# Two longer reckoned times in the planner of a hybrid decoder layer: low parts of weights on VectorE, wide operations on GpSimd

## The chip, the cores and the metric

The kernel runs on one core of a Trainium2 chip. A core has five engines, each with a queue of its own that it works through in order: TensorE (PE in the profile; its weight loads are PEld), VectorE (DVE), ScalarE (ACT), GpSimd (POOL) and SyncE (SP), which issues the weight transfers. The engines wait for each other by semaphores. The metric is the device time of one execution in microseconds; the figure before is the median of three runs.

## The reference, cut to what matters

One layer with 256 tokens of width 1024. A conditioning vector gives six vectors of shift, scale and gate. The normalised input goes through one product with 7168 columns, which feeds a convolution branch, an attention branch and two gates; their gated sum goes through `w_out`. Then 64 small experts, eight for each token, and a shared one.

```python
mod = c_act @ w_ada[l] + b_ada[l]                       # sh1, sc1, g1, sh2, sc2, g2
h = rms_norm(x, norm1_g[l]) * (1 + sc1) + sh1
ca, cb, q, k, v, gate_conv, gate_attn = jnp.split(h @ w_in[l], offsets, axis=-1)
u = causal_depthwise_conv(ca * sigmoid(cb), 31 taps) + b_dw
y_conv = silu(layer_norm(u)) @ w_pw2 + b_pw2
a = softmax(q1 k1) - lam * softmax(q2 k2)               # 8 heads, causal
y_attn = rms_norm(a @ v, subln_g)
x = x + g1 * ((sigmoid(gate_conv) * y_conv + sigmoid(gate_attn) * y_attn) @ w_out[l])
h2 = rms_norm(x, norm2_g[l]) * (1 + sc2) + sh2
x = x + g2 * moe_ffn(h2, ...)                           # top 8 of 64 experts, one shared
```

All is float32.

## The kernel before, in words

**How it is laid out.** The program has two parts. In the first, the weights of `w_in`, `w_pw2` and `w_out` come in 18 chunks of 512 columns (the list `SEQ`: `i0` to `i13`, `p0`, `p1`, `o0`, `o1`), each in eight blocks of 128 rows, which makes 144 work items. In the second, the experts' weights (3 MB for each expert) are streamed through slots of 1 MB. The first six experts are fixed; which weights come after them is known only when the routing has ordered the experts by their load, in `order_ids` (`ids`, line 1364).

**Split weights.** To multiply at float32 accuracy with a faster matmul, each weight block is split in two: ScalarE casts it to a high part (line 795), and a subtraction gives the low part (`lo_part`, line 776), on GpSimd or on VectorE. TensorE then runs twelve matmuls for an item (lines 802 to 804 for outputs with tokens in rows, 811 to 813 for outputs with channels in rows). Four buffers of high and low parts (two in the tile `ra`, two in `rb`) are in use up to the chunk `p1`, eight for the last two chunks.

**The convolution** (`conv`, lines 859 and 863) runs on VectorE: for each of four pairs of channel blocks one first tap and 30 more for each block, 248 instructions in all, accumulating in a PSUM bank; the last tap of a pair is written to `fa`. `layer_norm` adds up the channels (lines 1102 and 1108), subtracts the mean (1115), squares on ScalarE (1117), adds the squares (1125), takes the root on GpSimd (1132), broadcasts it over TensorE (1135, 1138), scales (1143), applies SiLU on ScalarE (1149) and splits the result into parts for the product with `w_pw2` (1152, 1154).

**Attention** (`attn`) runs in six groups: scores on TensorE (1012, 1016), row maxima on VectorE (1023), exponentials on ScalarE (1027), reciprocals and the factor lambda (1031, 1034, 1037), the combination of both softmaxes on VectorE (1040), transposes (1046) and their copy (1049), the product with v (1057), squares (1066), sums and root (1069, 1071, 1073), scaling (1075), transposes (1079), the gate (1084).

**What sets the order.** A planner written in Python (`Plan`) runs when the kernel is built. Each piece of work is a generator that yields requests: an engine with a time that the planner reckons for it (`GT(n)` for a GpSimd operation of n columns, `TT(n)` for a two-input operation on VectorE, and so on), an event or a buffer. The planner keeps a clock for each engine, takes the request that can start first by its own clock (with priorities `PRIO` among those that start within 0.02 us), and writes the instruction out; so the reckoned times set the order in every engine's queue. Where a request names two engines, the one that would be done first is taken, with a penalty if one is given: `lo_part` asks for GpSimd or VectorE, and VectorE gets a penalty of 1.0 us (`LO_BIAS`) once the convolution's second block of input is ready. `conv` has the lowest priority. The emitted queues are fixed; on the chip an engine that reaches an instruction whose input is late waits, with all that is behind it.

`GT(n)` is used for the low parts of weights (512 columns), the gain of q and k (line 928), the sums of the layer norm (256), the merge of the two branches, the residual sums and the split of the normalised tokens. `TT(512)` is 0.07 + 0.00104 x 512 = 0.60 us.

Of the kernel before, what the change touches and what calls it, by code (L numbers as in the profile page):

```python
# [166 lines left out]
LO_BIAS, Q_BIAS = (0.0, 1.0), 3.0  # L167
# [4 lines left out]
def TT(n):  # L172
    return "D", 0.07 + 0.00104 * n
# [16 lines left out]


def GT(n):
    return "G", 0.15 + 0.0021 * n


def MM(n):
# [4 lines left out]
def tile_hybrid_block(ctx, tc, x, c, positions, w_ada, b_ada, norm1_g, w_in, conv_dw, conv_dw_b,  # L201
# [4 lines left out]
    P, T, D, K = 128, 256, 1024, 8  # L206
# [6 lines left out]
    pl = Plan()  # L213
# [218 lines left out]
    def done(key, q, now=None):  # L432
        now = pl.cur.ready if now is None else now
        w = loaded[key]
        if w.off[q] in halves:
            e = halves.pop(w.off[q])
            load(*e, [1], now)
            advance(now)
        elif w.off[q] in once:
            once.remove(w.off[q])  # L440
        elif w.off[q] == LAST:
            w2s.close()
            obs = ctx.enter_context(tc.tile_pool(name="obs", bufs=1)).tile([P, 8 * KB], F32R, name="obs")
            pl.put("ob", *(ob_of(obs[:, i * D:(i + 1) * D]) for i in range(2)))
        else:
            pl.pools["w"].append((now, w.off[q]))
            advance(now)
# [324 lines left out]
    step = [0]  # L772

    def lo_part(i, hl, w, k):
        e = yield [GT(512), TT(512) + (None, LO_BIAS[pl.ev("u", 1).t is not None])]
        (nc.gpsimd if e == "G" else nc.vector).tensor_tensor(hl[:, 1], w.k[k], hl[:, 0].bitcast(F32),  # L776
                                                             op=OP.subtract)
        pl.set("hl", i)
        w.left[k // 4] -= 1
        if not w.left[k // 4]:  # L780
            done(w.key, k // 4)
# [4 lines left out]
    def splits(chunks):  # L786
        for i, (c_, k) in enumerate(items):
            key = chunks[c_][0]
            yield pl.ev("L", *key, k // 2)
            w = loaded[key]  # L790
            w.left, w.key = [4, 4] if not k else w.left, key
            yield w.at[k]
            hl = yield Get("hl")
            yield AS(512)
            nc.scalar.copy(hl[:, 0], w.k[k])  # L795
            pl.events["buf", i] = hl
            pl.spawn(lo_part(i, hl, w, k))
# [98 lines left out]
    def fin_qk(which, half):  # L896
        def qk_out(o, t):
# [23 lines left out]
            else:  # L921
# [3 lines left out]
            pl.put("s8", sm_)  # L925
            yield pl.ev("angles")
            e = yield [GT(512), TT(512) + (None, Q_BIAS)]
            (nc.gpsimd if e == "G" else nc.vector).tensor_tensor(
                q3, q3, qkg[:, which, None, :].to_broadcast([P, 8, 64]), op=OP.mult)
# [167 lines left out]
    def layer_norm():  # L1097
        yield pl.ev("cv", 0)
        for k in range(1, 6):
            yield pl.ev("cv", k)  # L1100
            e = yield [GT(256), TT(256) + (None, LO_BIAS[1])]
            (nc.gpsimd if e == "G" else nc.vector).tensor_tensor(lns, lns if k > 1 else cv[:, 0], cv[:, k], op=OP.add)
# [898 lines left out]
```

## Time and profile before

| | us |
|---|---|
| median of three runs (818.65 to 822.19) | 820.47 |
| the profiled execution | 819.49 |
| its span, from the first to the last instruction | 817.7 |
| TensorE busy | 766.1 (94%) |
| VectorE busy | 444.6 (54%) |
| ScalarE busy | 324.9 (40%) |
| GpSimd busy | 192.4 (24%) |

The profile shows one execution. Its shares are means over both parts of the program: 271.04 MB are moved in the span, at 420 GB/s or so in the second part and at 155 to 365 GB/s in the first. A busy TensorE is not one at its peak, since matmul ends are modelled. In the timelines an instruction can begin before the one ahead of it has ended, so durations add up to more than the time seen as busy. Times inside a run are counted from the start of the span.

### The profile page before, as it was taken

How to read it: one execution, taken by the hardware profiler on the slowest of the kernel's cores; microseconds unless marked ns; L12 is line 12 of the kernel's file. 1: busy time of each engine (PE TensorE's matmuls, PEld its weight loads, DVE VectorE, ACT ScalarE, POOL GpSimd, SP SyncE). 2: the span in 40 equal slices, each digit the busy share in tenths (PEclk: the TensorE clock that was granted, in tenths of full speed). 3: DMA queues.
4: the chain of work that ended last, by engine and by line, in shares of the span. 5: the costliest groups of instructions: out<-in, count | busy, mean ns of one | idle time of the engine just before them, and what ended most of it. 6: DMA issues, size and time to landing. Idle time of an engine off the chain costs nothing.

```text
span 817.7 us, 13180 instructions
## 1 busy us (share of the span) xinstructions
PE 766.1 (94%) x4759; PEld 469.8 (57%) x4759; DVE 444.6 (54%) x1035; ACT 324.9 (40%) x713; POOL 192.4 (24%) x246
## 2 busy tenths in 40 slices
PE   3999999899996999999999797999999999999997
PEld 2898777589784987545454141354464455444543
DVE  5458998999996677433433141344344344433443
ACT  4356656865759755223221021232232232232220
POOL 3003788888572693000002000000000000000000
PEclk9999999899997999989999898999999999999999
DMA  9998776546654676469999999999999999999993
GB/s 312 365 336 288 261 253 227 180 161 227 228 184 155 239 280 252 165 245 390 390 420 420 422 421 420 421 422 420 420 421 422 421 420 421 420 421 419 419 413 139
DMA packets 69883, 271.04 MB, mean 331 GB/s; under 512 B 6085, under 2 KB 15893, under 8 KB 46520
## 3 DMA queue, kind: packets, MB, share of 16 engines
q1 hardware_dynamic: 69464, 270.00, 84.9%
q8 instruction: 38, 0.62, 0.3%
q0 software_dynamic: 304, 0.16, 0.1%
q14 instruction: 29, 0.24, 0.1%
q10 hardware_dynamic: 48, 0.01, 0.0%
HBM read 269.11 MB, written 1.05 MB: 330 GB/s over the span
## 4 chain that ended last, share of the span: by engine, by line


## 5 line engine op out<-in xcount | busy, mean ns | idle before, releaser
L1802 PE MATMUL bank<-fa 128*32 128x512 f32 (+2 forms) x1048 | 203.7, 608 | 8.3 <-DMA fa<-in_w_exp_gu_dram 8.3
L1802 PEld LDWEIGHTS bank<-fa 128*32 128x32 f32 (+2 forms) x1048 | 60.3, 124 | 132.1 <-issue 107.3
L863 DVE SCALAR_TENSOR_TENSOR bank<-fa,tap,bank 128x256 f32<-128x256 f32 x232 | 112.9, 486 | 6.1
L1676 DVE SCALAR_TENSOR_TENSOR fa<-bank,gsc,h 128x256 f32<-128x256 f32 x28 | 13.5, 484 | 170.1 <-ACT h L1672 170.1
L1849 PE MATMUL bank<-fa 128*32 128x512 f32 (+1 forms) x496 | 83.9, 596 | 0.0
L1672 ACT ACTIVATE h<-bank 128x256 f32<-128x256 f32 x28 | 10.8, 385 | 179.7 <-PE bank L1802 179.7
L776 POOL TENSOR_TENSOR rb<-fa,rb 128x512 fp32r<-128x512 f32 x46 | 60.2, 1317 | 65.6 <-ACT rb L795 64.6
L1694 DVE TENSOR_TENSOR fa<-bank,fa 128x512 f32<-128x512 f32 x54 | 37.4, 692 | 65.5 <-PE bank L1849 62.7
L776 POOL TENSOR_TENSOR ra<-fa,ra 128x512 fp32r<-128x512 f32 x48 | 63.9, 1339 | 20.5 <-ACT ra L795 17.1
L1762 ACT CAST obs<-fa 128x512 fp32r<-128x512 f32 x54 | 33.4, 618 | 83.7 <-DVE fa L1694 83.7
L1719 DVE TENSOR_TENSOR fa<-fa,bank 128x512 f32<-128x512 f32 x108 | 66.7, 678 | 0.0
L1491 ACT ACTIVATE fa<-bank,b2c,a2c 128x256 f32<-128x256 f32 x108 | 53.6, 561 | 20.8 <-PE bank L1523 20.8
L795 ACT CAST ra<-fa 128x512 fp32r<-128x512 f32 x76 | 46.8, 622 | 37.0 <-PE bank L812 22.9
L1523 PE MATMUL bank<-ra 128*128 128x256 f32 x448 | 60.5, 288 | 0.0
L1710 PE MATMUL bank<-obs,ra 128*128 128x512 f32 x216 | 58.3, 412 | 0.0
L795 ACT CAST rb<-fa 128x512 fp32r<-128x512 f32 x68 | 42.0, 623 | 37.8 <-PE bank L812 22.4
L1802 PE MATMUL bank<-late_w,fa 128*32 128x512 f32 (+2 forms) x168 | 51.9, 627 | 4.1 <-DMA late_w<-in_w_exp_gu_dram 4.1
L1523 PEld LDWEIGHTS bank<-ra 128*128 128x128 f32 x448 | 55.6, 191 | 0.2
L1710 PEld LDWEIGHTS bank<-obs,ra 128*128 128x128 f32 x216 | 38.7, 188 | 28.8 <-issue 21.5
L811 PE MATMUL bank<-ra 128*128 128x256 f32 x160 | 47.8, 299 | 1.9 <-ACT ra L577 1.8
L1849 PEld LDWEIGHTS bank<-fa 128*32 128x32 f32 (+1 forms) x496 | 22.8, 119 | 41.1 <-issue 35.3
L811 PE MATMUL bank<-ra,rb 128*128 128x256 f32 x160 | 46.1, 288 | 0.0
(376 smaller groups left out, 1391.5 us busy)
## 6 DMA issues: line engine op xcount, KB each, us to landing
fa<-in_w_exp_gu_dram SPq DMA_DIRECT2D x100, 1024.0 KB, 19.8
fa<-in_w_exp_down_dram SPq DMA_DIRECT2D x50, 1024.0 KB, 19.8
fa<-in_w_ada_dram SPq DMA_DIRECT2D x24, 1024.0 KB, 7.9
fa<-in_w_in_dram SPq DMA_DIRECT2D x22, 1024.0 KB, 5.3
late_w<-in_w_exp_gu_dram SPq DMA_DIRECT2D x17, 1024.0 KB, 19.3
late_w<-in_w_exp_down_dram SPq DMA_DIRECT2D x12, 1024.0 KB, 6.8
fa<-in_w_exp_gu_dram SPq DMA_DIRECT2D x22, 512.0 KB, 9.4
fa<-in_w_in_dram SPq DMA_DIRECT2D x12, 512.0 KB, 9.4
```

What stands on the lines that cost most here:

```text
L776: (nc.gpsimd if e == "G" else nc.vector).tensor_tensor(hl[:, 1], w.k[k], hl[:, 0].bitcast(F32), op=OP.subtract)
L795: nc.scalar.copy(hl[:, 0], w.k[k])
L811: nc.tensor.matmul(o, hl[:, 0, mm], src_t[:, k, 0], start=(k == 0 and m % 2 == 0), stop=False)
L863: nc.vector.scalar_tensor_tensor(cv[:, m] if j == TAPS - 1 else acc, u_sb[:, m, j:j + T], tap[:, m, j:j + 1], acc, op0=OP.mult, op1=OP.add)
L1491: nc.scalar.activation(xt[:, k, 0:ns], p3[:, f2, 0:ns], AF.Identity, bias=b2c[:, k:k + 1], scale=a2c[:, k:k + 1])
L1523: nc.tensor.matmul(p3[:, f2, 0:ns], xr[:, a, t, (f + f2) * P:(f + f2 + 1) * P], tables[b0][:, t, 0:ns], start=(f2 + t + a == 0), stop=(f2 ...
L1694: nc.vector.tensor_tensor(o32, pd[h], g2b[:, h * 512:(h + 1) * 512], op=OP.mult)
L1710: nc.tensor.matmul(p, info.pT[:, t * P:(t + 1) * P], ob[a], start=(a == 0), stop=(a == 1))
L1719: nc.vector.tensor_tensor(x_sb[:, t, d], x_sb[:, t, d], p, op=OP.add)
L1762: nc.scalar.copy(ob[0], o32)
L1802: nc.tensor.matmul(pg[o:o + m], info.xt[:, k, o:o + m], loaded["g", js[e]].k[k], start=(k == 0), stop=(k == K - 1))
L1849: nc.tensor.matmul(pd[h][o:o + m], info.aT[:, f, o:o + m], loaded["d", js[e]].k[f][:, h * 512:(h + 1) * 512], start=(f == 0), stop=(f == 1))
```

## The change

Two numbers that the planner reckons with are changed. A GpSimd operation of n columns is taken to last 0.15 + 0.0023 n us, where it was 0.15 + 0.0021 n: 1.33 in place of 1.23 us for 512 columns, 0.74 in place of 0.69 for 256. The low part of a weight block on VectorE is taken to last 0.85 us, where it was 0.60; its penalty stays. No instruction is added or taken out by hand; the planner writes another order.

```diff
@@ -190,7 +190,7 @@
 def GT(n):
-    return "G", 0.15 + 0.0021 * n
+    return "G", 0.15 + 0.0023 * n
@@ -772,7 +772,7 @@
     def lo_part(i, hl, w, k):
-        e = yield [GT(512), TT(512) + (None, LO_BIAS[pl.ev("u", 1).t is not None])]
+        e = yield [GT(512), ("D", 0.85) + (None, LO_BIAS[pl.ev("u", 1).t is not None])]
         (nc.gpsimd if e == "G" else nc.vector).tensor_tensor(hl[:, 1], w.k[k], hl[:, 0].bitcast(F32),
                                                              op=OP.subtract)
```

In the new order 56 of the 144 low parts are on VectorE, where there were 50, and four operations of 256 columns go the same way (one of line 1102, one of 1125, two of 1154). ScalarE loads its function tables three times less. SyncE's queue is the same. From the residual sums on (line 1202), the queues differ by one scaling of tokens (line 1237) and its neighbours. Between the first of the convolution and the layer norm nearly every queue differs. Three places follow; in the names a number behind `bank_` tells which PSUM bank is meant.

VectorE in the third pair of channel blocks, before:

```order
L1075 TENSOR_TENSOR fa<-bank_76,mx 128x512
L776 TENSOR_TENSOR rb<-fa,rb 128x512
L863 SCALAR_TENSOR_TENSOR bank_78<-fa,tap,bank_78 128x256 x24
L764 TENSOR_TENSOR p_231<-bank_77,pcol 64x8
L863 SCALAR_TENSOR_TENSOR bank_78<-fa,tap,bank_78 128x256
L766 SCALAR_TENSOR_TENSOR a2c<-p_231,pcol 64x8
L863 SCALAR_TENSOR_TENSOR bank_78<-fa,tap,bank_78 128x256 x15
L863 SCALAR_TENSOR_TENSOR fa<-fa,tap,bank_78 128x256 x2
L1102 TENSOR_TENSOR fa<-fa 128x256
```

The same pair in the new order:

```order
L863 SCALAR_TENSOR_TENSOR bank_75<-fa,tap,bank_75 128x256 x22
L776 TENSOR_TENSOR rb<-fa,rb 128x512
L764 TENSOR_TENSOR p_231<-bank_74,pcol 64x8
L863 SCALAR_TENSOR_TENSOR bank_75<-fa,tap,bank_75 128x256
L766 SCALAR_TENSOR_TENSOR a2c<-p_231,pcol 64x8
L863 SCALAR_TENSOR_TENSOR bank_75<-fa,tap,bank_75 128x256 x5
L776 TENSOR_TENSOR ra<-fa,ra 128x512
L863 SCALAR_TENSOR_TENSOR bank_75<-fa,tap,bank_75 128x256
L776 TENSOR_TENSOR rb<-fa,rb 128x512
L863 SCALAR_TENSOR_TENSOR bank_75<-fa,tap,bank_75 128x256 x13
L1084 SCALAR_TENSOR_TENSOR fa<-bank_78,sl_213,fa 128x4x128
L863 SCALAR_TENSOR_TENSOR bank_75<-fa,tap,bank_75 128x256
```

More low parts (line 776) stand among the taps (line 863), and the gate of an attention group (line 1084) stands ahead of the pair's end.

VectorE around the last tap of the convolution, before (line 863 into `fa` is the last tap):

```order
L863 SCALAR_TENSOR_TENSOR bank_77<-fa,tap,bank_77 128x256 x5
L863 SCALAR_TENSOR_TENSOR fa<-fa,tap,bank_77 128x256 x2
L1110 TENSOR_SCALAR fa<-bank_78 128x256
L1115 TENSOR_TENSOR fa<-fa 128x256 x5
L1023 TENSOR_REDUCE mx<-bank_74 128x2
L1031 RECIPROCAL mx<-mx 128x2x2
L1115 TENSOR_TENSOR fa<-fa 128x256
L1034 TENSOR_SCALAR mx<-mx,lam 128x2
L1023 TENSOR_REDUCE mx<-bank_77 128x2
L1115 TENSOR_TENSOR fa<-fa 128x256 x2
L1125 TENSOR_TENSOR fa<-fa 128x256 x2
```

And in the new order:

```order
L863 SCALAR_TENSOR_TENSOR fa<-fa,tap,bank_75 128x256 x2
L1031 RECIPROCAL mx<-mx 128x2x2
L1034 TENSOR_SCALAR mx<-mx,lam 128x2
L1110 TENSOR_SCALAR fa<-bank_73 128x256
L1040 SCALAR_TENSOR_TENSOR fa<-fa,mx 128x256
L1115 TENSOR_TENSOR fa<-fa 128x256
L1040 SCALAR_TENSOR_TENSOR fa<-fa,mx 128x256
L1115 TENSOR_TENSOR fa<-fa 128x256 x7
L1125 TENSOR_TENSOR fa<-fa 128x256 x4
L1069 TENSOR_REDUCE mx<-fa 128x2
L1125 TENSOR_TENSOR fa<-fa 128x256
L1071 TENSOR_SCALAR mx<-mx 128x2
```

The row maxima of two groups (line 1023) no longer stand behind the last tap; one group's combination and sums (1040, 1069, 1071) still do.

TensorE between the layer norm's sum of squares (line 1128) and the first product with `w_pw2` (line 811), before; the rows go on with scores of the sixth group until line 811:

```order
L1128 MATMUL bank_78<-ones,fa 128x1 x2
L749 MATMUL bank_80<-fa,sel_111 128x512
L1057 MATMUL bank_76<-fa 128x128 x4
L1138 MATMUL bank_78<-fa,ones 128x128 x2
L1046 MATMUL bank_73<-ident,fa 128x128 x4
L1079 MATMUL bank_76<-ident,fa 128x128 x2
L1057 MATMUL bank_73<-fa 128x128 x4
L1012 MATMUL bank_74<-fa 128x256
```

And in the new order:

```order
L1079 MATMUL bank_80<-ident,fa 128x128 x2
L1108 MATMUL bank_73<-fa,ones 128x256 x2
L1046 MATMUL bank_79<-ident,fa 128x128 x4
L1057 MATMUL bank_79<-fa 128x128 x4
L1128 MATMUL bank_73<-ones,fa 128x1 x2
L1079 MATMUL bank_79<-ident,fa 128x128 x2
L1138 MATMUL bank_73<-fa,ones 128x128 x2
L811 MATMUL bank_78<-ra 128x256
L812 MATMUL bank_78<-ra 128x256
```

The scores of the sixth group (line 1012) are gone from here to an earlier place, and the broadcast (line 1138) is followed at once by the first product.

## Rows read from the trace of the kernel before

**Rows 1.** Busy time in stretches of 20 us. Columns: the stretch in us, its length, then busy us of TensorE, of its weight loads, of VectorE, ScalarE and GpSimd, each with its count of instructions, the granted TensorE clock as a share of full speed, the busy share of the DMA engines and GB/s.

```profile
...
80.00:100.00 20.00, 20.00 (x93) 14.76 (x86) 19.19 (x42) 12.65 (x23) 15.18 (x12) 1.00 0.76 267
...
220.00:240.00 20.00, 19.87 (x165) 18.90 (x164) 19.54 (x43) 11.36 (x22) 14.00 (x13) 1.00 0.52 165
...
400.00:420.00 20.00, 20.00 (x121) 9.52 (x122) 6.76 (x18) 6.44 (x14) 0.00 (x0) 1.00 1.02 424
...
780.00:800.00 20.00, 19.95 (x106) 7.62 (x100) 8.29 (x15) 3.60 (x7) 0.00 (x0) 1.00 1.02 403
```

**Rows 2.** The timeline of VectorE where the order of the experts is written: start in us, duration, engine, line, operation, written and read.

```profile
...
335.82 0.20 DVE L1364 CAST ids<-bank 1x64 int32<-1x64 f32 x1
```

**Rows 3.** Busy time in stretches cut by events: from the convolution's first tap to the ends of its four channel pairs, from the last tap to the first product of `w_pw2`, and from there to `ids`. Columns as in rows 1.

```profile
...
69.76:114.22 44.46, 43.40 (x239) 33.49 (x238) 42.28 (x86) 28.53 (x62) 34.33 (x37) 1.00 0.73 253
114.22:158.28 44.06, 40.14 (x196) 30.63 (x195) 38.75 (x85) 30.16 (x83) 37.56 (x62) 0.90 0.63 216
158.28:199.38 41.10, 41.02 (x276) 33.69 (x277) 38.07 (x85) 24.87 (x57) 32.90 (x46) 0.94 0.64 215
199.38:242.77 43.39, 42.24 (x340) 37.30 (x339) 42.05 (x90) 29.36 (x68) 28.72 (x25) 1.00 0.61 207
242.77:265.92 23.15, 15.51 (x76) 9.67 (x75) 15.79 (x45) 20.45 (x51) 6.96 (x8) 0.78 0.39 138
265.92:336.00 70.08, 67.65 (x435) 59.08 (x434) 50.70 (x129) 39.05 (x84) 39.31 (x34) 1.00 0.66 240
```

**Rows 4.** VectorE's groups of instructions from 69.76 to 242.77 us, different shapes apart: line, engine, operation, written and read with shapes, count, then busy us, mean ns of one, and idle time before them.

```profile
...
L776 DVE TENSOR_TENSOR ra<-fa,ra 128x512 fp32r<-128x512 f32 x8 | 8.7, 1084 | 1.1 <-ACT ra L795 1.1
L776 DVE TENSOR_TENSOR rb<-fa,rb 128x512 fp32r<-128x512 f32 x7 | 7.4, 1061 | 1.2 <-POOL fa L939 1.2
...
L1023 DVE TENSOR_REDUCE mx<-bank 128x2 f32<-128x512 f32 x4 | 2.7, 681 | 0.0
...
L1040 DVE SCALAR_TENSOR_TENSOR fa<-fa,mx 128x256 f32<-128x256 f32 x2 | 1.7, 836 | 0.0
...
L1102 DVE TENSOR_TENSOR fa<-fa 128x256 f32<-128x256 f32 x1 | 1.1, 1072 | 0.0
L1084 DVE SCALAR_TENSOR_TENSOR fa<-bank,sl,fa 128x256 f32<-128x256 f32 x1 | 0.5, 471 | 0.0
L1075 DVE TENSOR_TENSOR fa<-bank,mx 128x256 f32<-128x256 f32 x1 | 0.4, 418 | 0.0
L1069 DVE TENSOR_REDUCE mx<-fa 128x2 f32<-128x256 f32 x1 | 0.4, 413 | 0.0
...
L1034 DVE TENSOR_SCALAR mx<-mx,lam 128x2 f32<-128x2 f32 x1 | 0.2, 223 | 0.0
```

**Rows 5.** VectorE's timeline inside the convolution: a long run of taps, and a single tap between two other instructions.

```profile
...
176.22 12.55 DVE L863 SCALAR_TENSOR_TENSOR bank<-fa,tap,bank 128x256 f32<-128x256 f32 x24
...
217.59 0.48 DVE L1040 SCALAR_TENSOR_TENSOR fa<-fa,mx 128x256 f32<-128x256 f32 x1
217.99 0.48 DVE L863 SCALAR_TENSOR_TENSOR bank<-fa,tap,bank 128x256 f32<-128x256 f32 x1
218.38 1.19 DVE L1040 SCALAR_TENSOR_TENSOR fa<-fa,mx 128x256 f32<-128x256 f32 x1
```

**Rows 6.** The instructions of line 776, the low parts, from 69.76 to 242.77 us: engine, operation, count, duration in ns as least, median and most, first and last start.

```profile
...
L776 POOL TENSOR_TENSOR ra<-fa,ra x35: 1267/1293/1740, 75.9 to 239.9; 128x512 fp32r<-128x512 f32 x35
...
L776 DVE TENSOR_TENSOR ra<-fa,ra x8: 682/960/1854, 70.2 to 203.0; 128x512 fp32r<-128x512 f32 x8
```

**Rows 7.** Timelines from the last tap to the first product of `w_pw2`: TensorE, VectorE, ScalarE, and TensorE again. In brackets the idle time before, and what ended it.

```profile
...
242.43 1.13 PE L1108 MATMUL bank<-fa,ones 128*128 128x256 f32 x4 [0.30 <-DVE fa L863]
...
243.60 0.42 DVE L1110 TENSOR_SCALAR fa<-bank 128x256 f32<-128x256 f32 x1 [0.83 <-PE bank L1108]
...
253.70 0.16 DVE L1130 TENSOR_SCALAR lnc<-bank 128x2 f32<-128x2 f32 x1 [1.10 <-PE bank L1128]
254.89 0.48 DVE L1135 TENSOR_SCALAR fa<-ident,lnc 128x128 f32<-128x128 f32 x2 [1.03 <-POOL lnc L1132]
...
258.36 0.42 DVE L1069 TENSOR_REDUCE mx<-fa 128x2 f32<-128x256 f32 x1 [1.47 <-ACT fa L1066]
...
248.82 1.28 ACT L975 ACT_TABLE_LOAD   x1
...
263.71 2.08 PE L1012 MATMUL bank<-fa 64*128 64x256 f32 x8
```

**Rows 8.** TensorE's timeline in the products of `w_pw2` (lines 811 to 813) up to the first of `w_out` (line 802).

```profile
...
265.92 0.36 PE L811 MATMUL bank<-ra 128*128 128x256 f32 x1
...
281.64 1.16 PE L1057 MATMUL bank<-fa 128*128 128x128 f32 x8 [0.47 <-ACT fa L1049]
...
288.69 0.28 PE L811 MATMUL bank<-ra,rb 128*128 128x256 f32 x1
...
290.13 0.28 PE L811 MATMUL bank<-ra,rb 128*128 128x256 f32 x1
...
291.57 0.39 PE L802 MATMUL bank<-ra,mt 128*128 128x512 f32 x1
```

**Rows 9.** Granted clock at the first product of `w_pw2`, and after a hole later on. Columns as in rows 1.

```profile
...
265.00:266.00 1.00, 1.00 (x7) 0.30 (x5) 0.71 (x3) 1.00 (x4) 0.80 (x1) 0.56 0.00 0
...
350.00:355.00 5.00, 4.94 (x14) 1.54 (x16) 0.23 (x1) 0.01 (x1) 0.00 (x0) 0.54 0.03 10
```

## The prediction

> **What bounds the kernel now.** I read the busy time in stretches of 20 us first, since the shares over the whole span mix two programs [rows 1]. From 400 us on the DMA engines are full (share 1.02, 424 GB/s) and stay so to 800 us, and VectorE and ScalarE are busy for a third of the time: the 64 experts' weights are streamed in. Before that DMA is at half to three quarters, and at 80 to 100 us and 220 to 240 us both TensorE (20.00 and 19.87 of 20) and VectorE (19.19 and 19.54) are full. So the second part runs at the memory's pace and the change can touch only its start. That start hangs on one small result, the order of the experts (`ids`, line 1364, at 335.82 us [rows 2]): all expert loads but the first six experts' need it, and the slots for them come free only as the first experts are computed, which waits for the same routing. I take a shift of `ids` as a shift of the end, one for one.
>
> What sets `ids`? I cut the first part at the ends of the convolution's four channel pairs and at the first product after the layer norm [rows 3]. From 69.76 to 242.77 us, 173.0 us, VectorE is busy for 42.28 + 38.75 + 38.07 + 42.05 = 161.1 us: the convolution with all that is put between its taps is VectorE's, and the layer norm waits for its last tap. Then come 23.15 us in which every engine has holes (VectorE 15.79 busy, TensorE 15.51): a chain of dependent steps. From 265.92 us TensorE is busy 67.65 of 70.08 us: the products of `w_pw2` and `w_out`, norm and routing. So three terms: VectorE's work up to the last tap, the chain after it, TensorE's work after that.
>
> **The change, part by part.** The two numbers touch no instruction, only where the planner puts it. A low part on VectorE is now reckoned at 0.85 us, in place of 0.60; it measures 1.08 and 1.06 in this window [rows 4]. GpSimd's is reckoned at 1.33, in place of 1.23. Low parts on VectorE get no rarer by it: they go from 50 to 56, since GpSimd's became dearer too, and four operations of 256 columns go the same way. More than that moves: attention steps that stood behind the last tap now stand ahead of it.
>
> *VectorE up to the last tap.* Counting the rows of the order from the first tap to the last, and pricing each with its mean in that window [rows 4], it gains: 5 of the 6 low parts at 1.07 = 5.35; 4 row maxima (line 1023) at 0.68 = 2.72; 4 combinations of two softmaxes (line 1040, 256 wide) at 0.84 = 3.34; 2 each of lines 1069, 1075 and 1084 at 0.41, 0.42 and 0.47 = 2.60; one sum of line 1102 at 1.07; and 2 each of lines 1031, 1034 and 1071, which are narrow, at up to 0.22 = 1.3. Together 16.4 us. Neighbouring instructions overlap a little: the groups of the window sum to 172 us of which 161.1 are seen as busy, a factor of 0.94, so 15.4 us. Back again comes a little where a run of taps is cut: 24 taps in a row take 12.55 us, 0.52 each, but a tap that stands alone lets the next instruction start 0.39 later [rows 5]. The runs go from 64 to 74, which gives 10 x 0.13 = 1.3 us back: 14.1 us. That is the upper end, since the means hold waits: a low part on VectorE takes 0.68 us at the least and up to 1.85 us [rows 6], and GpSimd, busy 133.5 of these 173 us [rows 3], has five fewer in the new order. With the least for low parts and the 0.48 us of a quiet line 1040 [rows 5] for lines 1040 and 1102 it is 12.4 x 0.94 - 1.3 = 10.4 us. I take 12.5, nearer the upper end because GpSimd stays busy for over 70% of the window.
>
> A rule speaks against adding to VectorE just here. The Trainium skill ("SBUF — State Buffer", Who interferes with whom) has it that a VectorE instruction with two inputs in SBUF and a GpSimd instruction that reads SBUF exclude each other, and the second to issue waits for the whole of the first. The trace agrees in kind, with the 1.85 us beside 0.68. If each of the five met a full GpSimd operation (0.68 + 1.29 = 1.97 us, an estimate), the sum would be 4.2 us longer.
>
> TensorE gives no room to hide this: at 242.43 us it has run out of its own products and waits for the last tap [rows 7]. In the new order it has one more attention group to do before the layer norm, 4 to 6 us; the tap at about 255 us still comes last.
>
> *The chain after the last tap.* Before, three attention groups are woven into it: ScalarE changes its table for them (1.28 us a time), TensorE's sum for the mean square and its broadcast stand behind attention matmuls, and the first product waits behind the scores of a sixth group, 2.08 us [rows 7]. Now only the end of one group is left in it. I add the steps from the rows, with T the last tap's end: mean at T + 0.8 (0.83 before line 1110), two combinations and eight subtractions to T + 5.9, the squares' sums to T + 8.4, line 1130 at T + 9.6 (1.1 through TensorE), GpSimd's root and the diagonals to T + 11.3 (1.2 and 0.5), the first scaling at T + 12.3, eight of them to T + 15.3, the first low part to T + 15.7, so the first product can run at about T + 16.5. Against 23.15 that is 6.6 us less. The bounds: 15 (8.1 less) if nothing waits, 19 (4.1 less) if the remaining group's steps each wait as they do now.
>
> *TensorE after it.* The sixth group's transposes and value products leave the projection stretch: among them a product of 1.16 us with a wait of 0.47 us [rows 8]. The 16 work items of `w_pw2` took from 265.92 to 291.57 us, 25.65 us; one item of twelve matmuls takes 1.44 (288.69 to 290.13), so 16 are 23.0. Of the 2.6 us left I let 2.1 go. Against it, the products now start after a longer rest. At 265 us the granted clock was 0.56, mostly the lower level of 1.2 GHz, while attention matmuls ran ahead of the first product; without these the first products themselves run at the lower level, as after the hole at 345 us, where the clock was 0.54 for 5 us [rows 9]. 1.0 us, between 0 and 2.3. The routing tail is the same but for one shift of 0.3 us, left out.
>
> *Sum.* 12.5 - 6.6 - 2.1 + 1.0 = +4.8 us. The profiled execution took 819.5 us and the median of the runs is 820.5; on their middle, 820.0, this gives **824.8 us**.
>
> **The rivals.** *A wash.* The same three terms at their friendly ends: 10.4 - 8.1 - 2.1 + 0 = 0.2, so 820. For it: GpSimd has less to do in the window, and the chain is freer. Against: half of the low parts in the window are held up now (of the eight in `ra` the median is 0.96 us against a least of 0.68 [rows 6]).
>
> *Faster.* Besides that, VectorE stops waiting inside the convolution. 11.9 of the 173 us are not busy [rows 3], part of it waits for steps that the planner thought done, as costs too low let it think. With truer costs half may go: 820 - 6 = 814. It decides by one point: if the last tap ends before 251 us (242.8 + 6.6 + 2.1 - 1.0 = 250.5), the new order wins. Against it: VectorE already is the engine behind its plan, so it mostly finds its inputs ready.
>
> *Slower still.* Near the last tap the new order has attention steps in close sequence (lines 1040, 1069, 1075, 1084), each of which needs a round trip over TensorE, ScalarE or GpSimd, with few taps between; a queue in order then holds the taps behind it. In the chain now such waits are 0.8 to 1.5 us each [rows 7]; five of them and the full exclusion of the low parts give 824.8 + 7 = 832.
>
> *Nothing of this counts.* If the expert stream were held by something other than `ids`, time would stay at 820; I count it with the wash.
>
> **How the numbers follow.** The forecast has 0.50 (it spans 822 to 829), the wash 0.23, faster 0.15, slower still 0.12. The range reaches from 817 to 832 us, which leaves out most of the faster case and the end of the slower. A measurement of this kernel tells about 0.5% (4.1 us) from no change. Slower than that: 0.36 of the forecast's 0.50, all 0.12 of the last, 0.02 of the wash, 0.50. Same: 0.14 + 0.20 + 0.01 = 0.35. Faster: 0.15.
>
> **What would show it.** In the changed kernel's profile the last tap (line 863 into `fa`) should end at 253 to 258 us; the first product of line 811 after it 15 to 19 us later; the first product of line 802 from `mt` 23 to 25 us after that; `ids` at 338 to 345 us; and from 400 us on 420 GB/s as before. I am wrong in the first term if VectorE is busy for no longer than now (161 us) in the convolution and the tap ends by 250 us; wrong in the second if TensorE's own products, not the last tap, end last; wrong in the frame if `ids` moves and the end does not.

## The result, and the profile after

| | before | after |
|---|---|---|
| median, us | 820.66 (818.65 to 822.99, 6 runs) | 826.52 (824.98 to 828.87, 6 runs) |
| span of the profiled execution, us | 817.7 | 824.3 |
| VectorE busy, us | 444.6 | 452.0 |
| GpSimd busy, us | 192.4 | 184.9 |
| TensorE busy, us | 766.1 | 764.4 |

The ratio is 1.0068 [1.0048, 1.0087]: 5.9 us slower between the medians, where 4.8 were forecast. Here and below two far slower executions, one of e3 (1247 us) and one of e10 (1494 us), are left out of the medians.

The same cut by events as in [rows 3], of the kernel after: first tap, ends of the four channel pairs, last tap, first product of `w_pw2`, and on to `ids`. Columns as there.

```profile
...
68.17:114.70 46.53, 46.13 (x253) 35.87 (x252) 44.35 (x87) 31.29 (x72) 38.13 (x46) 1.00 0.73 256
114.70:160.94 46.24, 45.81 (x243) 34.27 (x243) 40.50 (x97) 33.56 (x97) 38.82 (x64) 0.96 0.71 246
160.94:205.75 44.81, 44.81 (x336) 39.15 (x335) 40.28 (x82) 27.43 (x66) 33.55 (x41) 0.96 0.57 191
205.75:255.19 49.44, 39.81 (x284) 32.47 (x283) 47.95 (x106) 32.15 (x74) 21.38 (x18) 0.89 0.64 222
255.19:270.86 15.67, 8.11 (x27) 5.34 (x26) 9.91 (x32) 7.23 (x17) 4.10 (x4) 0.50 0.26 77
270.86:343.87 73.01, 68.68 (x418) 60.22 (x419) 52.34 (x127) 37.96 (x78) 36.25 (x29) 0.95 0.55 199
```

VectorE where the order of the experts is written (it answers to [rows 2]):

```profile
...
343.67 0.20 DVE L1364 CAST ids<-bank 1x64 int32<-1x64 f32 x1
```

And the second part, in the same columns as [rows 1]:

```profile
...
400.00:420.00 20.00, 20.00 (x131) 8.82 (x124) 5.83 (x12) 4.67 (x10) 0.00 (x0) 1.00 1.01 423
```

Put beside the rows of before, the profiled executions differ so:

| stretch | before | after | difference | forecast |
|---|---|---|---|---|
| start to first tap | 69.76 | 68.17 | -1.6 | 0 |
| first tap to last tap | 173.0 | 187.0 | +14.0 | +12.5 |
| last tap to first product | 23.15 | 15.67 | -7.5 | -6.6 |
| first product of `w_pw2` to first of `w_out` | 25.65 | 25.54 | -0.1 | -2.1 + 1.0 |
| from there to `ids` | 44.25 | 47.27 | +3.0 | 0 |
| `ids` to the end | 481.9 | 480.6 | -1.2 | 0 |

The first row is no effect of the change: in another execution with before's order the first tap stood at 68.19 (e6, below). Single executions of one order differ. Two of the runs below keep the order of before (e6) and of after (e7) up to the first product of `w_pw2`. Their convolutions, and those of e3 and e4, read so, columns as in [rows 1], in the order e6, e7, e3, e4:

```profile
...
68.19:244.81 176.62, 170.99 (x1047) 138.79 (x1045) 161.41 (x341) 113.16 (x268) 133.04 (x169) 0.93 0.63 219
...
71.06:256.64 185.58, 175.44 (x1111) 140.54 (x1110) 173.29 (x368) 124.59 (x304) 132.43 (x167) 0.96 0.67 231
...
68.19:242.52 174.33, 166.83 (x1047) 135.14 (x1045) 162.56 (x346) 113.05 (x268) 127.12 (x164) 0.96 0.65 222
...
69.44:255.03 185.59, 175.48 (x1111) 140.58 (x1110) 171.81 (x363) 124.83 (x304) 136.82 (x172) 0.96 0.66 231
```

In one order VectorE's busy time repeats within some 0.3 us (161.2 and 161.4 before, 173.1 and 173.3 after), but its idle time does not (11.9 and 15.2, 13.9 and 12.3). So the convolution's +14.0 is +9.0 between the other two executions, while VectorE's busy time there is +11.9 in both pairs, and the last tap's end moves by 12.4 us (242.77 to 255.19) and 11.8 (244.81 to 256.64). The chain after the tap repeats (23.2 in both of before's order, 15.7 in both of after's). Of these terms only what exceeds some 3 us, or shows again in other kernels, is read as an effect.

**What the convolution is made of now.** VectorE's groups between first and last tap after, columns as in [rows 4]:

```profile
...
L776 DVE TENSOR_TENSOR rb<-fa,rb 128x512 fp32r<-128x512 f32 x11 | 10.2, 924 | 1.9 <-ACT rb L795 1.9
L776 DVE TENSOR_TENSOR ra<-fa,ra 128x512 fp32r<-128x512 f32 x9 | 8.3, 922 | 1.3 <-ACT ra L795 1.3
L1023 DVE TENSOR_REDUCE mx<-bank 128x2 f32<-128x512 f32 x8 | 5.5, 681 | 0.0
...
L906 DVE TENSOR_SCALAR s<-s 128x8 f32<-128x8 f32 x8 | 4.9, 608 | 0.0
...
L1040 DVE SCALAR_TENSOR_TENSOR fa<-fa,mx 128x256 f32<-128x256 f32 x6 | 4.2, 697 | 0.0
L1040 DVE SCALAR_TENSOR_TENSOR fa<-fa,mx 128x128 f32<-128x128 f32 x8 | 3.6, 449 | 0.0
...
L1102 DVE TENSOR_TENSOR fa<-fa 128x256 f32<-128x256 f32 x2 | 1.9, 950 | 0.0
...
L1084 DVE SCALAR_TENSOR_TENSOR fa<-bank,sl,fa 128x256 f32<-128x256 f32 x3 | 1.4, 480 | 0.2 <-PE bank L1079 0.2
...
L1075 DVE TENSOR_TENSOR fa<-bank,mx 128x256 f32<-128x256 f32 x3 | 1.2, 413 | 0.0
L1069 DVE TENSOR_REDUCE mx<-fa 128x2 f32<-128x256 f32 x3 | 1.2, 411 | 0.0
```

Before, two groups that are not in [rows 4] read so:

```profile
...
L1040 DVE SCALAR_TENSOR_TENSOR fa<-fa,mx 128x128 f32<-128x128 f32 x8 | 3.9, 490 | 0.0
...
L906 DVE TENSOR_SCALAR s<-s 128x8 f32<-128x8 f32 x8 | 2.8, 351 | 0.0
```

Group by group: the row maxima (+2.8 us) and lines 1069, 1075 and 1084 (together +2.5) grew as priced, line 1040 by 2.2 in both shapes and not by 3.34, line 1102 by 0.8 and not by 1.07. The low parts grew from 8.7 + 7.4 = 16.1 to 18.5, by 2.4 and not by 5.35: there are five more of them, but each takes 0.92 us in place of 1.07. Line 906, a scaling of 8 columns that the change doesn't touch, grew by 2.1: its count is the same, its mean went from 351 to 608 ns. VectorE's idle time in the window went from 11.9 us to 187.02 - 173.08 = 13.9, which is inside its scatter.

**The chain and the products.** TensorE and VectorE from the last tap on, in the form of [rows 7]:

```profile
...
254.85 2.08 PE L1108 MATMUL bank<-fa,ones 128*128 128x256 f32 x4 [4.18 <-DVE fa L863]
...
264.92 1.01 PE L1128 MATMUL bank<-ones,fa 128*128 128x1 f32 x4 [2.35 <-DVE fa L1125]
...
267.70 1.22 PE L1138 MATMUL bank<-fa,ones 128*128 128x128 f32 x4 [0.77 <-DVE fa L1135]
270.86 0.58 PE L811 MATMUL bank<-ra 128*128 128x256 f32 x1 [1.94 <-ACT ra L1152]
272.09 0.58 PE L812 MATMUL bank<-ra 128*128 128x256 f32 x1 [0.65 <-DVE ra L1154]
...
272.68 0.41 PE L811 MATMUL bank<-ra 128*128 128x256 f32 x1
...
273.32 0.41 PE L811 MATMUL bank<-ra 128*128 128x256 f32 x1
...
256.97 0.42 DVE L1110 TENSOR_SCALAR fa<-bank 128x256 f32<-128x256 f32 x1 [1.42 <-PE bank L1108]
```

TensorE waits 4.18 us for the last tap, so the convolution still comes last. Its waits behind that (2.35, 0.77 and 1.94 us) are for the chain's own steps; only one group's end is left beside them, and VectorE's wait for the mean grew from 0.83 to 1.42. The granted clock is 0.50, the lower level of 1.2 GHz, over the whole chain. The first products run at that level too: three matmuls take 0.64 us (272.68 to 273.32). From 275 us the clock is back:

```profile
...
275.20 0.28 PE L811 MATMUL bank<-ra 128*128 128x256 f32 x1
275.55 0.28 PE L811 MATMUL bank<-ra 128*128 128x256 f32 x1
```

Three matmuls take 0.35 there. So two things cancel. From 270.86 to 275.20, in 4.34 us, five threes run, which at 0.36 each take 1.8: 2.5 us are lost, 0.65 of them in a wait for the low part (line 1154). The other 59 of the 64 threes take 21.2 us, 0.36 each: no attention product stands among them any more, and that gains the 2.6 us that lay beside 23.0 before.

**Behind `w_out`.** The 3.0 us that were not forecast begin at the merge of the two branches. VectorE, and TensorE that waits:

```profile
...
297.00 2.52 DVE L1178 TENSOR_TENSOR fa<-fa 128x256 f32<-128x256 f32 x2
299.45 1.79 DVE L776 TENSOR_TENSOR ra<-fa,ra 128x512 fp32r<-128x512 f32 x1
301.16 2.95 DVE L1182 TENSOR_TENSOR mt<-fa,mt 128x256 fp32r<-128x256 f32 x2
...
304.82 0.74 DVE L1178 TENSOR_TENSOR fa<-fa 128x256 f32<-128x256 f32 x2
...
305.71 0.69 PE L802 MATMUL bank<-ra,mt 128*128 128x512 f32 x1 [1.79 <-ACT mt L1180]
...
330.56 0.66 PE L1243 MATMUL bank<-ident,fa 128*128 128x128 f32 x4 [1.49 <-DVE fa L1237]
```

Two operations of 256 columns take 2.52 us, two others 2.95, where two take 0.74 at 304.82, with a low part of 1.79 us between: all are held up. Before, one such pair took as long, and TensorE did not wait:

```profile
...
294.74 2.96 DVE L1178 TENSOR_TENSOR fa<-fa 128x256 f32<-128x256 f32 x2
```

Now `mt` is late, and TensorE waits 1.79 us for it; before, its only waits from the first `w_out` product to `ids` were 0.65 and 1.16 us, at line 1243. That wait is 1.49 now.

### The profile page after: what moved, and what is told of

The parts are those of the page before. It is cut to its first block, busy times and chain, and to the rows that moved or that the text cites. A ratio compares the mean times of both kernels' runs of the same rounds, so it can differ in the third digit from the quotient of the medians.

```text
span 824.3 us, 13177 instructions
## 1 busy us (share of the span) xinstructions
PE 764.4 (93%) x4759; PEld 472.3 (57%) x4759; DVE 452.0 (55%) x1045; ACT 322.2 (39%) x710; POOL 184.9 (22%) x236
## 4 chain that ended last, share of the span: by engine, by line
## 5 line engine op out<-in xcount | busy, mean ns | idle before, releaser
L1802 PE MATMUL bank<-fa 128*32 128x512 f32 (+2 forms) x1048 | 201.8, 604 | 10.6 <-DMA fa<-in_w_exp_gu_dram 10.6
L1672 ACT ACTIVATE h<-bank 128x256 f32<-128x256 f32 x28 | 10.8, 385 | 179.6 <-PE bank L1802 179.6
L776 POOL TENSOR_TENSOR rb<-fa,rb 128x512 fp32r<-128x512 f32 x42 | 55.7, 1333 | 76.0 <-ACT rb L795 72.3
L776 POOL TENSOR_TENSOR ra<-fa,ra 128x512 fp32r<-128x512 f32 x46 | 61.7, 1350 | 27.2 <-ACT ra L795 25.5
L1523 PE MATMUL bank<-ra 128*128 128x256 f32 x448 | 60.7, 288 | 0.0
L811 PE MATMUL bank<-ra 128*128 128x256 f32 x160 | 47.7, 298 | 3.8 <-ACT ra L1152 1.9
L812 PE MATMUL bank<-ra 128*128 128x256 f32 x160 | 46.9, 293 | 0.7 <-DVE ra L1154 0.6
## 6 DMA issues: line engine op xcount, KB each, us to landing
fa<-in_w_exp_gu_dram SPq DMA_DIRECT2D x100, 1024.0 KB, 19.8
fa<-in_w_exp_down_dram SPq DMA_DIRECT2D x50, 1024.0 KB, 19.8
```

The lines of the kernel that those rows point to most:

```text
L811: nc.tensor.matmul(o, hl[:, 0, mm], src_t[:, k, 0], start=(k == 0 and m % 2 == 0), stop=False)
L812: nc.tensor.matmul(o, hl[:, 0, mm], src_t[:, k, 1], start=False, stop=False)
L1523: nc.tensor.matmul(p3[:, f2, 0:ns], xr[:, a, t, (f + f2) * P:(f + f2 + 1) * P], tables[b0][:, t, 0:ns], start=(f2 + t + a == 0), stop=(f2 ...
L1802: nc.tensor.matmul(pg[o:o + m], info.xt[:, k, o:o + m], loaded["g", js[e]].k[k], start=(k == 0), stop=(k == K - 1))
```

## The experiments

All kernels in one table. "Ahead of the tap" counts low parts on VectorE, row maxima and combinations of softmaxes between the first tap and the last; the next columns are the profiled execution's stretches (first to last tap, last tap to first product, first product to `ids`, `ids` to end); the ratio is to the kernel before, timed on the same chip.

| kernel | ahead of the tap | taps | chain | to `ids` | to end | median | ratio |
|---|---|---|---|---|---|---|---|
| before | 15, 8, 10 | 173.0 | 23.2 | 69.9 | 481.9 | 820.7 | 1 |
| after | 20, 12, 14 | 187.0 | 15.7 | 72.8 | 480.6 | 826.5 | 1.0068 [1.0048, 1.0087] |
| e1 | 24, 12, 13 | 186.4 | 15.6 | 71.1 | 482.3 | 828.8 | 1.0115 [1.0082, 1.0148] |
| e2 | 11, 8, 12 | 176.6 | 21.2 | 71.6 | 481.7 | 820.9 | 1.0005 [0.9983, 1.0028] |
| e3 | 20, 8, 10 | 174.3 | 23.4 | 70.6 | 482.4 | 822.0 | 1.0026 [1.0002, 1.0051] |
| e4 | 15, 12, 14 | 185.6 | 15.7 | 73.9 | 481.2 | 826.8 | 1.0075 [1.0047, 1.0102] |
| e5 | 20, 6, 10 | 178.9 | 27.4 | 73.3 | 481.2 | 832.6 | 1.0117 [1.0088, 1.0145] |
| e6 | 15, 8, 10 | 176.6 | 23.2 | 77.6 | 481.1 | 828.5 | 1.0070 [1.0039, 1.0101] |
| e7 | 20, 12, 14 | 185.6 | 15.7 | 72.5 | 482.4 | 827.1 | 1.0055 [1.0034, 1.0076] |
| e8 | 6, 4, 6 | 165.2 | 19.8 | 87.5 | 481.1 | 823.7 | 1.0024 [1.0007, 1.0041] |
| e9 | 10, 12, 14 | 183.6 | 14.1 | 72.2 | 481.6 | 821.9 | 1.0030 [1.0005, 1.0056] |
| e10 | 13, 10, 12 | 179.6 | 16.1 | 71.4 | 484.1 | 819.4 | 0.9982 [0.9962, 1.0002] |
| e11 | 9, 8, 8 | 168.0 | 24.4 | 73.4 | 481.0 | 821.0 | 1.0008 [0.9982, 1.0034] |
| e12 | 30, 12, 16 | 188.1 | 13.8 | 70.8 | 481.8 | 827.2 | 1.0094 [1.0070, 1.0118] |

### e1 and e2: each number alone

```diff
-    return "G", 0.15 + 0.0021 * n
+    return "G", 0.15 + 0.0023 * n
```

> Only GpSimd's reckoned time is raised. The order then has 60 low parts on VectorE, 24 of them between the first and the last tap (15 before, 20 with both numbers), and four more row maxima there, as with both. Theory A (VectorE's work ahead of the last tap sets the layer norm's start, and the freer chain gives part of it back): 9 x 1.07 + 2.7 + 2.5 + 1.5 + 1.1 + 0.8 = 18.2 us, x 0.94 - 18 cuts x 0.13 = 14.8 us later, the last tap at about 257 us, 7 us given back in the chain: 827 to 829 us. Theory B (low parts on VectorE are hidden, only the order of attention costs): as with both numbers, 826.5 us.

```diff
-        e = yield [GT(512), TT(512) + (None, LO_BIAS[...])]
+        e = yield [GT(512), ("D", 0.85) + (None, LO_BIAS[...])]
```

> Only the reckoned time of the low part on VectorE is raised. The order then has 43 low parts on VectorE, 11 of them ahead of the last tap (15 before), two more combinations and two more sums of line 1102, and as many row maxima as before. Theory A: -4 x 1.07 + 2 x 0.84 + 2 x 1.07 + 0.4 = -0.1 us, last tap at 241 to 244 us, time 819 to 822 us. A theory by which the dearer low part is the harmful number: 824 us or more.

GpSimd's longer time alone makes the kernel slower (1.0115); the longer low part alone makes no difference that can be told (1.0005). The change's loss comes from the first number. Both times lie where theory A put them, the last taps do not: 254.4 us for 257 in e1, 246.1 for 241 to 244 in e2.

### e3 and e4: the five low parts without the order, and the order without them

Before's order with the five low parts put on VectorE at their places, and the new order with the same five on GpSimd:

```diff
+        e = "D" if i in (75, 78, 88, 101, 103) else e
```

> The order of before, with five low parts inside the convolution (work items 75, 78, 88, 101 and 103) issued on VectorE in place of GpSimd, nothing else moved. It is the price of the moved low parts by themselves. Theory A: 5 x 1.07 x 0.94 - 5 x 0.13 = 4.4 us later at the last tap and at the end, 825 us; with waits at their least 2.5 us, 823 us. Theory B (hidden): 820.7 us.

```diff
+        e = "G" if i in (75, 78, 88, 101, 103) else e
```

> The changed order, with the same five low parts issued on GpSimd, nothing else moved. Theory A: the last tap comes 2.5 to 4.4 us earlier than 255.2 us, time 822 to 824 us, still above before. Theory B: 826.5 us as with the change.

Five low parts more lengthen the convolution by 1.3 us (173.0 to 174.3); five fewer in the new order shorten it by 1.4 us (187.0 to 185.6). Between single executions that is less than the scatter, but VectorE's busy time, which repeats, says the same: 1.2 to 1.4 us more in e3, 1.3 to 1.5 less in e4. By the times e3 (822.0) lies between its two theories, and e4 stays at 826.8, where theory B has it: with before's number of low parts on VectorE the whole loss is still there. The share that the forecast gave them (five at 1.07, 5.35 us) is too large. Where the rest goes shows in VectorE's groups of e4 (its lines stand one lower):

```profile
...
L777 DVE TENSOR_TENSOR rb<-fa,rb 128x512 fp32r<-128x512 f32 x8 | 8.3, 1040 | 2.1 <-ACT rb L796 2.1
L777 DVE TENSOR_TENSOR ra<-fa,ra 128x512 fp32r<-128x512 f32 x7 | 6.1, 873 | 0.6 <-ACT ra L796 0.6
L1041 DVE SCALAR_TENSOR_TENSOR fa<-fa,mx 128x128 f32<-128x128 f32 x8 | 5.6, 702 | 0.0
```

The low parts fall from 18.5 to 14.4 us, but the combinations of 128 columns rise from 3.6 to 5.6: with five more operations on GpSimd, other instructions of VectorE are held up in their place.

### e5: three attention groups kept behind the last tap

```diff
+        if (qt, h0) in GROUPS[3:]:
+            yield pl.ev("cv", 7)
```

> The changed numbers, and the last three attention groups may start only once the last tap is planned. The order then has 20 low parts on VectorE ahead of the last tap, as with the change, but 6 row maxima and 10 combinations there, where the change has 12 and 14 and before 8 and 10. Theory A2 (after the first runs: the attention steps ahead of the last tap are the loss, the five low parts cost 1.3 us): last tap at 242 to 246 us, the chain after it 20 to 24 us, time 819 to 823 us. Rival (the low parts and the dearer reckoning as such are the loss): last tap past 250 us, 826 us or more.

The expectation failed, and with it the reading that the steps pulled ahead of the tap are the loss whatever becomes of them. The convolution does get shorter by 8.1 us (187.0 to 178.9), about what the removed steps measure in the groups' rows (6 row maxima 4.1, 4 combinations 1.9, lines 1069, 1075 and 1084 2.5); VectorE's busy time there falls by 6.7, to 166.4. But the chain grows by 11.8 us. Here are TensorE (the kernel's lines from 1002 on stand two lower) and the chain's stretch, columns as in [rows 1]:

```profile
...
249.70 1.22 PE L1110 MATMUL bank<-fa,ones 128*128 128x256 f32 x2 [10.32 <-DVE fa L863]
...
277.47 0.58 PE L811 MATMUL bank<-ra 128*128 128x256 f32 x1 [4.47 <-ACT ra L1154]
```

```profile
...
250.03:277.47 27.44, 16.93 (x71) 11.35 (x70) 17.72 (x51) 14.40 (x45) 3.77 (x5) 0.62 0.30 96
```

TensorE has nothing to do for 10.32 us ahead of the tap, and then runs the groups' matmuls in the chain, at a granted clock of 0.62 where before's chain has 0.78 [rows 3]. In this order attention ahead of the tap costs less than behind it. That is no rule: e5 keeps more of it behind than before does (6 row maxima ahead, where before has 8), and before, with less ahead than the changed kernel, is faster than both.

### e6: `ids` late by itself

30 copies of 128 columns on VectorE ahead of `ids`, in the kernel before:

```diff
+        for _ in range(30):
+            nc.vector.tensor_copy(gov.rearrange("p t e -> p (t e)"), iot)
```

> The order of before, with 30 copies of 128 columns on VectorE directly ahead of the order of the experts, about 6 us in which nothing else is done there; the planner does not know of them. It tests the frame: if a shift of the order of the experts is a shift of the end, 826 to 827 us; if the stream of weights has slack there, 820.5 to 823 us.

```profile
...
337.88 7.79 DVE L1365 COPY fa<-iot 128x128 f32<-128x128 f32 x30
345.58 0.20 DVE L1366 CAST ids<-bank 1x64 int32<-1x64 f32 x1
```

`ids` comes 7.8 us later by the copies and the median is 7.4 us higher (821.18 to 828.53; the lines stand two lower). The expectation had the copies at 6 us. The frame of the prediction holds, and the table says the same: over 14 kernels with `ids` between 335.7 and 350.7 us, the time from there to the end is 480.6 to 484.1.

### e7: the low parts behind `w_out` as before

```diff
+        e = "D" if i in (134, 135) else e
+        e = "G" if i in (129, 132) else e
```

> The changed order, with two low parts of the last chunks (items 129 and 132) issued on GpSimd in place of VectorE, and two later ones (134 and 135) on VectorE, as before the change. It asks for the 3 us that the stretch from the first product of w_out to the order of the experts grew by. If the low parts hold up the merges on VectorE, TensorE's wait of 1.79 us for a cast of mt goes and the stretch shrinks from 47.3 to about 45.3 us: 824.5 us. If not, 826.5 us.

TensorE at its wait for `mt` (the lines stand two lower):

```profile
...
307.11 0.50 PE L804 MATMUL bank<-ra,mt 128*128 128x512 f32 x1 [0.95 <-ACT mt L1182]
```

The wait for `mt` is halved and not gone. From the first `w_out` product to `ids` it takes 45.8 us in place of 47.3 (44.25 before), but the time, 827.1, can't be told from 826.5. So the place of these four low parts makes at most half of the 3.0 us; what makes the rest stays open.

### e8: a dearer penalty, so fewer low parts on VectorE

```diff
-LO_BIAS, Q_BIAS = (0.0, 1.0), 3.0
+LO_BIAS, Q_BIAS = (0.0, 1.5), 3.0
```

> The numbers of before, with the penalty of low parts on VectorE at 1.5 in place of 1.0 us. The order then has 6 low parts, 4 row maxima and 6 combinations ahead of the last tap (15, 8 and 10 before). Theory A2, read the other way: -9 x 0.27 - 4 x 0.60 - 4 x 0.8 and their sums, 10 us less ahead of the last tap, which comes at 232 to 236 us, but the chain after it takes 25 to 30 us since four groups are woven into it: 815 to 821 us. If TensorE is short of low parts instead, its own products end after the last tap: 822 us or more.

The last tap comes at 236.25 us, 6.5 earlier than before, and the kernel is not faster: the second case of the expectation. The attention that is not done by then stands among the products of `w_pw2`, which take 35.5 us in place of 25.65. TensorE waits there for high and low parts:

```profile
...
267.17 0.39 PE L811 MATMUL bank<-ra 128*128 128x256 f32 x1 [2.99 <-ACT ra L795]
...
268.52 0.39 PE L813 MATMUL bank<-ra 128*128 128x256 f32 x1 [0.85 <-POOL ra L776]
```

Here an earlier last tap is worth nothing.

### e9 to e12: neighbouring numbers

The pair of numbers (GpSimd's time for a column, VectorE's low part) at (0.0019, 0.70), (0.0022, 0.85), (0.0022, 1.00) and (0.0024, 0.60); shown is the first:

```diff
-    return "G", 0.15 + 0.0021 * n
+    return "G", 0.15 + 0.0019 * n
...
-        e = yield [GT(512), TT(512) + (None, LO_BIAS[...])]
+        e = yield [GT(512), ("D", 0.70) + (None, LO_BIAS[...])]
```

> Both numbers moved the other way round: GpSimd at 0.0019 a column, the low part on VectorE at 0.70 us. In this order 10 low parts stand on VectorE between the first tap and the last (15 before, 20 in the changed kernel), but as many attention steps as in the changed kernel (12 row maxima, 14 combinations). Theory V (the loss is VectorE's whole load there, low parts and what meets them included): the convolution takes 173 + 8 - 2 = 179 us, the chain 16, so 820 to 822 us. Theory O (the loss is the attention steps pulled ahead): convolution 185 to 187, 825 to 828 us.

> GpSimd at 0.0022 a column, the low part on VectorE at 0.85 us: half of the first step of the change, all of the second. 13 low parts, 10 row maxima and 12 combinations ahead of the last tap. Theory V: convolution 175 to 178 us, chain 18 to 20, 820 to 822 us. A theory without a trend (each order is its own accident): anywhere from 818 to 830.

> GpSimd at 0.0022 a column and the low part on VectorE at 1.00 us, both near what the trace shows (1.29 us for 512 columns on GpSimd, 0.92 to 1.08 on VectorE). 9 low parts, 8 row maxima and 8 combinations ahead of the last tap. Theory V: convolution 168 to 171 us, chain 20 to 23; if TensorE then lacks no weights, 816 to 819; if it does, as in the run with the penalty of 1.5, 822 to 825.

> GpSimd at 0.0024 a column, the low part on VectorE at its old 0.60 us: 30 low parts, 12 row maxima and 16 combinations ahead of the last tap. Theory V: the steps from 15 to 20 to 24 low parts cost 6 and 8 us; 30 give 832 to 838 us. Theory O (attention steps only, 2 combinations more than in the changed kernel): 827 to 829.

Neither theory holds throughout. O fails at e9: as many attention steps ahead of the tap as in the changed kernel, and 821.9 us. V fails at e12: 30 low parts, and 827.2 us where it gave 832 to 838; from 15 to 30 low parts in orders with 12 row maxima ahead (e4, after, e12) the medians are 826.8, 826.5 and 827.2 (e1, with 24, has 828.8). It also gave too short a convolution for e9 and e10 (183.6 and 179.6), and e11's 821.0 lies between its two cases. In e11 the tap ends at 237.9 us, and TensorE, still at its own products, comes to the layer norm's sums only at 240.55, without a wait:

```profile
...
240.55 1.03 PE L1108 MATMUL bank<-fa,ones 128*128 128x256 f32 x4
```

What does hold over all fourteen, in the main, is that the convolution grows with the work that is put on VectorE there (165.2 us with 317 instructions, e8, to 188.1 with 380, e12; with the same 341 it took 173.0 and 176.6) and the chain shrinks as attention leaves it, while the two together range from 185.0 (e8) to 206.4 (e5). e10, with half of the step in GpSimd's number, is the lowest; its interval ends at 1.0002, so it is not shown to beat the kernel before.

## Why the prediction was right, point by point

**The frame** (`ids` sets the end) is shown, by e6 and by the last stretch in the table.

**VectorE up to the last tap**: forecast +12.5 us, bounds 10.4 and 14.1; measured +14.0, +9.0 between e6 and e7, and +11.9 of VectorE's busy time in both pairs; the tap ended at 255.19, inside 253 to 258. The size is right, the working only in part. The row maxima and lines 1069, 1075 and 1084 cost what their rows said; e5, which takes three groups out again, gets 8.1 us back. The low parts were mis-sized: their own busy time grew by 2.4 us for 5.35, and VectorE's as a whole by 1.2 to 1.5 for them (e3, e4). Line 1040 was priced 1.1 us too high, with a mean that holds waits. The price of a moved instruction was taken from what it lasts on the engine that gets it, and the engine that loses it was left out: GpSimd has five operations fewer, which hold up VectorE's other instructions less. The groups priced in the sum grew by 10.7 us (low parts, row maxima, line 1040, the three lines, line 1102) where it had 15.1; line 906, which it did not price, was held up 2.1 us more. That the sum, taken inside its bounds, still met the busy time is in part luck. The 2.0 us more idle time show nothing: the new order's other execution has 12.3 us of it, before's other one 15.2. So the mechanism of the rival "slower still", taps held behind attention steps that wait, isn't shown.

The rule cited from the Trainium skill ("SBUF — State Buffer", Who interferes with whom) would have made the sum 4.2 us longer if each of the five met a full GpSimd operation. They did not: the low parts' mean fell to 0.92 us. That such meetings happen the trace does show, after `w_out` (1.79 us beside 0.68).

**The chain**: forecast -6.6 us, bounds 8.1 and 4.1 less; measured -7.5, nearly the end at which nothing waits. That attention left it is what shortened it; e5 puts the groups back and it is 27.4 us.

**The products**: forecast -2.1 + 1.0, measured -0.1. The first `w_out` product came 25.54 us after the first of `w_pw2`, just outside the 23 to 25 of the forecast. Both effects are there and both are larger: the clock stayed at the lower level into the products, up to 275 us, which with the wait for the low part cost 2.5 rather than 1.0, and the attention's leaving gave 2.6 rather than 2.1.

**From `w_out` to `ids`**: forecast nothing (0.3 us left out), measured +3.0; e4, with the same order there, has 47.3 us again, and e6, with before's, takes 44.1 besides its 7.8 us of copies. This is the step that failed. The prediction called the routing tail the same but for one shift, which is true from the residual sums on; the merge of the branches and the low parts ahead of them were left out, and there VectorE is held up.

**The sum** came out close, +4.8 for +5.9 in the medians, since the missed 3.0 us were partly offset by the better chain and by what single executions scatter. That the misses cancelled so far is luck. Faster and the wash are ruled out for this order, by the time and by the point at which the first decides (a last tap by 251 us); so is "nothing of this counts", by e6. "Slower still" at its 832 us did not come.

**What stays open.** Which part of the new order is to blame can't be named in one term. It is not the five low parts: without them the whole loss is there (e4). Nor is it the count of attention steps ahead of the tap alone: with the same row maxima and combinations there and ten low parts fewer, e9 has convolution +10.6, chain -9.0 us and a median 1.5 us above before. The four low parts of e7 make no more than 1.5 us. The 6 us are a sum of such pieces, most of them within the scatter of single executions. Nor is it settled why e9 is 4.6 us faster than the changed kernel (3.1 by the ratios); in its profiled execution 3.4 of it lie in the convolution, where VectorE is busy as long as after (173.6 us to 173.1) and only idles less, 1.5 in the chain and 0.6 up to `ids`.

## What to carry to other kernels

When a planner moves an operation between two engines that hold each other up, price both ends: what it adds on the one, and the waits that go with it from the other (five low parts: 5.35 us by their own durations, 1.2 to 1.5 of VectorE's busy time). Follow the new order to the event that sets the end, not only to where the main rows differ: the earlier last tap of e8 was given back among the products of `w_pw2`, part of after's shorter chain behind `w_out`. And a planner's reckoned time is no slope: with the low part at 0.85, GpSimd's number at 0.0022 gives 819.4 us and at 0.0023 826.5, although both are near what the operation takes (1.28 and 1.33 us reckoned for 512 columns, a median of 1.29 [rows 6]), so neighbouring values are to be timed before one is kept.

## What the runs showed of the hardware that was not expected

In the profiled execution of e9 one low part on VectorE took 6.88 us, where it takes 0.68 undisturbed. VectorE, then GpSimd's operations under it, and TensorE, which waited for it:

```profile
...
162.34 6.88 DVE L776 TENSOR_TENSOR ra<-fa,ra 128x512 fp32r<-128x512 f32 x1
...
162.56 1.28 POOL L776 TENSOR_TENSOR rb<-fa,rb 128x512 fp32r<-128x512 f32 x1
...
164.38 1.29 POOL L776 TENSOR_TENSOR ra<-fa,ra 128x512 fp32r<-128x512 f32 x1
...
166.19 2.48 POOL L776 TENSOR_TENSOR rb<-fa,rb 128x512 fp32r<-128x512 f32 x2
168.63 0.64 POOL L912 TENSOR_TENSOR s<-s 128x8 f32<-128x8 f32 x1
...
169.27 0.58 PE L813 MATMUL bank<-ra 128*128 128x256 f32 x1 [3.20 <-DVE ra L776]
```

From 162.56 to 168.67 us GpSimd ran eight operations without a hole between them, at their usual durations, and VectorE's ended 0.55 us after the last of them; GpSimd's next one, of 8 columns, took 0.64 us where such ones take 0.20. It looks as if VectorE had to wait for the whole train and not for one operation. The other long low parts of these runs are 1.7 to 1.85 us, one operation's worth. This was seen once, and no run was made to test it.
